# Two-operand elementwise work of the middle stage goes from GpSimd to VectorE in a hybrid decoder step

## The chip, the cores and the metric

The kernel runs on one core of one Trainium2 chip. The metric is the device time of one execution in microseconds (us). Engines are called PE (TensorE matmul), PEld (its weight load), DVE (VectorE), ACT (ScalarE), POOL (GpSimd) and SP (SyncE, which here only issues DMAs).

## The reference

One layer (`DEPTH = 1`) is applied to a prompt of 1024 tokens and to a sample group of 8 single tokens; the kernel handles them as 1032 columns of one activation matrix.

```python
xn = _rms_norm(h, W['norm_g'][l])
zall = jnp.einsum('btd,de->bte', xn, W['w_in'][l])     # 1024 -> 5760 columns
# z_shift | g_a | u | v | g_b | m_a | m_b
y_a, S, last, v = _rwkv7(z_shift, ...)                 # 8 heads x 64, scan over tokens:
#   sa = S @ aa ; S = S*w + sa bb^T + v k^T ; y = S @ r ; then group norm and a bonus term
y_b = u * _chunk_spatial(layer_norm(gelu(v)))          # causal 128x128 mixing in chunks
br_a = (y_a * silu(g_a)) @ W['w_br_a'][l]
br_b = (y_b * silu(g_b)) @ W['w_br_b'][l]
h = h + (sigmoid(m_a) * br_a + sigmoid(m_b) * br_b) @ W['w_out'][l]
h = h + sigmoid(h @ W['w_ple_gate'][l] + b) * (p @ W['w_ple'][l])
y = _rms_norm(h, W['final_g'])
```

All results are float32.

## The kernel before

**Products in two parts.** A float32 product is made of three matmuls: each operand is split into a rounded part (hi) and a residual (lo), and hi·hi, hi·lo and lo·hi are added up in PSUM (line 138). `split` (line 111) makes the parts: ACT copies the raw tile into hi, then the engine that is handed in subtracts hi from raw to give lo (line 114). A block of weights, 128 output channels by 1024 inputs, comes in two slabs of 128x512 (`load_w`, line 116): a DMA into `wraw` issued by SP, the ACT cast `whi` (line 113), and the subtraction `wlo` on POOL. Three buffers of each slab tile exist, and a block uses its two slabs through all three thirds of the columns, so the second slab of the next block finds a free buffer only when the last third of the present block has passed its first half.

**Stages.** The first stage (lines 157 to 375) normalises the input and computes the v path. The middle stage (lines 377 to 1168) holds the RWKV branch with everything else woven in. The last stage (from line 1171) is three series of blocks, `w_br_a`, `w_out` and `w_gate`.

**The middle stage.** The recurrence is cut into 4 head pairs of two halves, 8 units (`un`), each of 8 chunks of 64 tokens. For a unit `stage_e` prepares the operands: decay powers `p65`, normalised keys `kn`, the matrices `m1` (tile `m1b`, two buffers, unit by unit) and `w3`. Line 663 writes the receptance products of `m1` (`zr` times the powers), line 665 the products of the normalised key. `stage_s` solves a triangular system per chunk, all chunks side by side, in 31 steps of two short DVE instructions (`xtmp` line 737, `xg` line 739). `stage_x` finishes it. `stage_c` then walks the 8 chunks in series: two PE products `pt` (line 827), an ACT copy, PE (line 833), two ACT copies, two PE products `p3b` (line 838), and on DVE the two halves of the state update that write `vsb` for the next chunk:

```python
V.scalar_tensor_tensor(nx, p3[Q[h], i % 2, h], pc[Q[h], c:c + 1], sp[Q[h]], ALU.mult, ALU.add)
```

The next chunk's `pt` needs `vsb`. `stage_t` puts a finished unit in place. `sample` does the recurrence of the 8 single tokens. Between these steps `Stream.pump` feeds PE with the matmuls of 49 weight blocks: 41 of `w_in` (13 `z`, 4 `ga`, 8 `u`, 16 gates) and 8 half-depth ones of `w_br_b`, 90 slabs in all.

**Order.** Every engine executes its instructions in one fixed order. A planner chooses it when the program is built, by a priority (the number of the instruction in the program, much lower and so more urgent for what goes through `Boost`, line 780: the chunk walk, `stage_t`, `load_yb`) and by when it expects operands to be ready. `st.lastv` is the newest DVE instruction made through `Boost`, mostly a state update. `tc.issue_after(x)` puts instructions behind x in their engine's order, with no wait for x to finish. It was already in use for every second step of `stage_s` (line 736) and for all DVE work of `sample` (line 919).

Of the kernel before, what the change touches and what calls it, by code (L numbers as in the profile page):

```python
# [10 lines left out]
ALU = mybir.AluOpType  # L11
# [16 lines left out]
CH = 64  # L28
# [26 lines left out]
def body(tc, A):  # L55
    nc = tc.nc
    V, S, G, SY = nc.vector, nc.scalar, nc.gpsimd, nc.sync
# [3 lines left out]
    f32 = lambda ap: ap.bitcast(F32)  # L61

    with ExitStack() as top:
# [47 lines left out]
        def split(hi, lo, eng, raw=None):  # L111
            raw = f32(lo) if raw is None else raw
            S.copy(hi, raw)  # L113
            eng.tensor_tensor(lo, raw, f32(hi), ALU.subtract)  # L114

        def load_w(src, nk, pool=None):
            out = []
            for k0 in range(0, nk, 4):
                n = min(4, nk - k0)
                x = k0 if pool else ""  # L120
                hi = (pool or wp).tile([P, 4, P], F32R, tag=f"whi{x}", name="whi")[:, :n]
                lo = (pool or wp).tile([P, 4, P], F32R, tag=f"wlo{x}", name="wlo")[:, :n]
                raw = (pool or wp).tile([P, 4, P], F32, tag="wraw", name="wraw", bufs=WRAW)[:, :n]
                SY.dma_start(raw, src[:, k0:k0 + n, :])
                split(hi, lo, G, raw)
                out += [(hi[:, k], lo[:, k]) for k in range(n)]
            return out

# [28 lines left out]
        with ExitStack() as es:  # L157
# [204 lines left out]
            for g in range(4):  # L362
                st = trp.tile([P, T], F32, tag="st", name="st_mix")
# [135 lines left out]
        def zblock(b, mk):  # L499
            def gen(w):  # L500
                z = mk()
                G.memset(z[:, 0:1], 0.0)

                def ev(n, ns, ps):
                    S.copy(z[:, 1 + n * W3:1 + (n + 1) * W3], ps)
                yield from mm_block(w, xhi, xlo, ev)

                def mix():
                    G.tensor_copy(zsh[:, b], z[:, TP:TP + NB + 1])
                    if b < 12:  # L510
                        zt.setdefault(b % 4, {})[b // 4] = z
                    mu = col("mu", b)
                    for n in (2, 1, 0):
                        c0 = 1 + n * W3
                        c1 = c0 + W3
                        d = r2.tile([P, W3], F32, tag="zd", name="zd")
                        e1 = min(c1, TP + 1)
                        V.tensor_tensor(d[:, :e1 - c0], z[:, c0 - 1:e1 - 1], z[:, c0:e1], ALU.subtract)
                        if n == 2:
                            V.tensor_tensor(d[:, e1 - c0:], shs[:, b], z[:, TP + 1:], ALU.subtract)  # L520
                        V.scalar_tensor_tensor(z[:, c0:c1], d, mu, z[:, c0:c1], ALU.mult, ALU.add)
                    if b < 12:
                        G.tensor_copy(zsm[:, (1, 0, 2)[b // 4], b % 4], z[:, TP + 1:])
                    else:
                        S.activation(z[0:64, 1:], z[0:64, 1:], AF.Tanh)
                        G.tensor_copy(wdas, z[:, TP + 1:])
                        for q, x, E_ in ((Q[0], lw, V), (Q[1], la, G)):
                            oq = Q[1 - q.start // 64]
                            S.copy(x[q], z[q, 1:])
                            E_.tensor_tensor(x[oq], z[q, 1:], f32(x[q]), ALU.subtract)  # L530
                if b // 4 != 1:
                    return mix
                mix()
            j, x = b % 4, b // 4
            go = {0: lambda: st.r_seen >= 2 * j, 1: lambda: st.k_seen >= 2 * j, 2: lambda: st.c_seen >= 2 * j - 4,
                  3: lambda: True}[x]
            st.add(("z", b), b, gen, ready=go if x != 1 else lambda: st.it >= 2 * j - 3, go=go)
# [38 lines left out]
        def lora_w(j):  # L576
            js = slice(j * P, (j + 1) * P)
            raw = wp.tile([P, 4, P], F32, tag="wraw", name="lraw", bufs=WRAW)[:, :2]
            for x in range(2):
                for h in range(2):  # L580
                    SY.dma_start(raw[Q[h], x], A["wup"][x * 64:x * 64 + 64, js])
            S.copy(lhi, raw)
            for x in range(2):
                G.tensor_tensor(llo[Q[x], x], raw[Q[x], x], f32(lhi[Q[x], x]), ALU.subtract)

        sgat, zt, ut, fin_s, tl = {}, {}, {}, {}, {}
        ybh, ybl = xhi[:, 0:4], xlo[:, 0:4]
# [2 lines left out]
        def stage_e(un):  # L590
# [54 lines left out]
            V.scalar_tensor_tensor(kp, zr[:, hs], col("r_k", j), kp, ALU.mult, ALU.mult)  # L645
            rkh = re_.tile([P, HT], F32R, tag="e_i", name="e_rkh")
            rkl = re_.tile([P, HT], F32R, tag="e_a", name="e_rkl")
            split(rkh, rkl, G, kp)
            yield YE[2]
            st.until(("z", 8 + j))  # L650
            if un == 0:
# [5 lines left out]
            for b0 in (0, 4):  # L657
# [2 lines left out]
                    yield 1  # L660
                for h in range(2):
                    q = Q[h]
                    G.tensor_tensor(m1[q, cs, h, RC[h]], c64(zr[q, hs])[:, cs], p65[q, cs, 1:], ALU.mult)
                    for b in range(2):
                        (G, V)[h].tensor_tensor(kord(m1[q, cs, h, AC[h]], b), perm(c64(kn[q])[:, cs], b),
                                                perm(p65[q, cs, 0:CH], b), ALU.mult)
                if b0:
                    st.r_seen += 1
                ps = aps().rearrange("p (c h x) -> p c h x", h=2, x=CH)
# [222 lines left out]
        def ugb(j, part):  # L892
            def gen(w):
                mx = trp.tile([P, T], F32, tag="st", name="mx")
                SY.dma_start(mx, (d_mix, d_yb)[part][j])

                def ev(n, ns, ps):
                    ue = r2.tile([P, W3], F32, tag="zd", name="ue")
                    if part == 0:
                        S.activation(ue, ps, AF.Gelu_apprx_tanh)  # L900
                    else:
                        S.activation(ue, ps, AF.Tanh, scale=0.5)
                        V.scalar_tensor_tensor(ue, ue, 1.0, ps, ALU.add, ALU.mult)
                    G.tensor_tensor(mx[:, ns], mx[:, ns], ue, ALU.mult)
                yield from mm_block(w, xhi, xlo, ev)
                SY.dma_start(d_yb[j], mx)
            st.add(("u", j, part), (17 if part == 0 else 25) + j, gen)
# [20 lines left out]
        def sample():  # L928
# [83 lines left out]
            yl = sa_(P, 32, tag="s_yl")  # L1012
            for r in range(2):
                it = []
                for x, E_ in enumerate((G, V)):
                    isl, s_ = sst[2 * r + x]
                    t_ = re_.tile([P, 8, HD], F32, tag=("e_a", "e_p")[x], name="s_t")
                    sa8 = r2.tile([P, 8], F32, tag="s_sa", name="s_sa")
                    E_.tensor_tensor(t_, s_, bi(lv[:, NKK]), ALU.mult)
                    it.append((E_, isl, s_, t_, sa8))  # L1020
                yield YS[0]
                for E_, isl, s_, t_, sa8 in it:
                    V.tensor_reduce(sa8, t_, AX.X, ALU.add)
                    E_.tensor_tensor(s_, s_, bi(lv[:, WV]), ALU.mult)
                    E_.tensor_tensor(t_, bj(sa8), bi(lv[:, BV]), ALU.mult)
                    E_.tensor_tensor(s_, s_, t_, ALU.add)
                    E_.tensor_tensor(t_, bj(lvv[:, isl]), bi(lv[:, KP]), ALU.mult)
                    E_.tensor_tensor(s_, s_, t_, ALU.add)
                    E_.tensor_tensor(t_, s_, bi(lv[:, RV]), ALU.mult)
                yield YS[1]  # L1030
                for E_, isl, s_, t_, sa8 in it:
                    V.tensor_reduce(yl[:, isl], t_, AX.X, ALU.add)
                yield 1
                while r == 0 and st.cdone < 7 * HCH + 3:
                    yield 1
# [36 lines left out]
        def load_ya(n):  # L1072
            ns = slice(n * W3, min((n + 1) * W3, TP))
            st.load = SY.dma_start(f32(yal[:, :3, ns]), d_ya[:3, :, ns].rearrange("k p t -> p k t")).ins
            for k in range(3):
                st.later.append(lambda k=k, ns=ns: split(yah[:, k, ns], yal[:, k, ns], G))

        def load_yb(n):
            V, S, G_ = (Boost(e) for e in (nc.vector, nc.scalar, nc.gpsimd))
            ns = slice(n * W3, (n + 1) * W3)  # L1080
            SY.dma_start(f32(ybl[:, :, ns]), d_yb[:, :, ns].rearrange("k p t -> p k t"))
            for k in range(4):
                S.copy(ybh[:, k, ns], f32(ybl[:, k, ns]))
                (G_ if k == 1 else V).tensor_tensor(ybl[:, k, ns], f32(ybl[:, k, ns]), f32(ybh[:, k, ns]), ALU.subtract)

        def br_b(j):
            def gen(w):
# [11 lines left out]
        fill += [lambda j=j: mgate(37 + j, d_mb[j]) for j in range(KD)]  # L1099
        fill += [lambda j=j: mgate(29 + j, d_ma[j]) for j in range(KD)]  # L1100

        tc.cur_priority = 100000
        boost[0] = 50000
        zblock(12, lambda: re_.tile([P, T + 1], F32, tag="zr", name="wda"))
# [61 lines left out]
            pass  # L1166
        repool.__exit__(None, None, None)
        rw.close()
        use_pmm(4)

        tr2 = top.enter_context(tc.tile_pool(name="tr2", bufs=2))
# [219 lines left out]
```

## Time and profile before

| | us |
|---|---|
| median of 3 runs (lowest, highest) | 1077.36 (1076.85, 1077.84) |
| the profiled execution | 1079.88 |
| its span, first to last instruction | 1078.0 |
| PE busy | 1016.7 (94%) |
| PEld busy | 978.4 (91%) |
| DVE busy | 655.1 (61%) |
| ACT busy | 449.3 (42%) |
| POOL busy | 471.6 (44%) |

The profiled execution has 1.9 us outside its span. Busy time is the union of an engine's instructions. PE at 94% counts overlapping matmuls, so the idle rest is a lower bound of what PE loses. The slices of the profile page show PE at 6 to 9 tenths throughout, DVE busiest in the first two thirds, and the granted clock of PE at full speed but for single slices.

### The profile page before, as it was taken

What the parts mean: (1) busy time and instruction counts of PE and PEld (TensorE: products, weight loads), DVE (VectorE), ACT (ScalarE), POOL (GpSimd) and SP (SyncE); (2) the same over time, 40 slices, a digit from 0 to 9 for tenths busy, and PEclk for the clock granted to TensorE, in tenths of its full rate; (3) what the DMA queues carried; (4) which work ended last, traced back from release to release, by engine and by line L of the source; (5) the groups of instructions that cost most, each with busy time, mean ns of one, the idle gap of its engine ahead of it and who ended that gap; (6) DMA issues with size and microseconds to landing.
All of it is one profiled execution on the core that took longest, in us unless ns stands there. A gap on an engine that the chain in (4) does not pass through costs nothing. (4 is left out here: it accounts for less than half of the span.)

```text
span 1078.0 us, 17989 instructions
## 1 busy us (share of the span) xinstructions
PE 1016.7 (94%) x6590; PEld 978.4 (91%) x6590; DVE 655.1 (61%) x1487; ACT 449.3 (42%) x1087; POOL 471.6 (44%) x484
## 2 busy tenths in 40 slices
PE   8889999899798999989998999999899999999996
PEld 8768898899798899989998999989799999999995
DVE  6898565847648768577476583563876551114544
ACT  4531334245364453555444545434532232225431
POOL 2462665444364343343414333334943674453213
PEclk9999999999899999999998999999899999999997
DMA  9811412152224231132232332422765763224204
GB/s 277 243 51 48 145 40 58 40 131 83 79 78 151 79 86 61 47 103 56 79 110 49 105 101 70 134 86 41 266 206 179 240 231 118 79 83 133 80 1 157
DMA packets 95224, 118.72 MB, mean 110 GB/s; under 512 B 40672, under 2 KB 61024, under 8 KB 95136
## 3 DMA queue, kind: packets, MB, share of 16 engines
q1 hardware_dynamic: 95136, 117.57, 35.5%
q8 instruction: 52, 0.85, 0.3%
q14 instruction: 36, 0.29, 0.1%
HBM read 84.75 MB, written 32.25 MB: 109 GB/s over the span
## 5 line engine op out<-in xcount | busy, mean ns | idle before, releaser
L138 PE MATMUL mm<-xhi,wlo 128*128 128x344 f32 x1176 | 388.2, 330 | 8.0 <-POOL wlo L114 6.2
L138 PE MATMUL mm<-xlo,whi 128*128 128x344 f32 x1176 | 389.3, 331 | 0.9 <-DVE xlo L791 0.8
L138 PE MATMUL mm<-xhi,whi 128*128 128x344 f32 x1176 | 388.7, 331 | 0.4 <-DVE mb L1092 0.3
L114 POOL TENSOR_TENSOR wlo<-wraw,whi 128x512 fp32r<-128x512 f32 x130 | 171.2, 1319 | 217.6 <-ACT whi L113 215.6
L138 PEld LDWEIGHTS mm<-xhi,wlo 128*128 128x128 f32 x1176 | 225.1, 191 | 10.5 <-POOL wlo L114 7.3
L138 PEld LDWEIGHTS mm<-xlo,whi 128*128 128x128 f32 x1176 | 224.9, 191 | 3.0 <-DVE xlo L791 1.7
L138 PEld LDWEIGHTS mm<-xhi,whi 128*128 128x128 f32 x1176 | 224.9, 191 | 2.6 <-DVE mb L1092 0.6
L113 ACT CAST whi<-wraw 128x512 fp32r<-128x512 f32 x130 | 80.2, 619 | 61.8 <-PE mm L138 44.4
L737 DVE TENSOR_TENSOR xtmp<-nb,xg 128x48 f32<-128x48 f32 (+23 forms) x248 | 70.6, 285 | 20.4 <-DMA nb<-d_n 13.6
L739 DVE TENSOR_TENSOR xg<-xg,xtmp 128x48 f32<-128x48 f32 (+23 forms) x248 | 78.0, 315 | 7.6 <-DVE xtmp L737 0.2
L791 ACT ACTIVATE sp<-vsb,pc 64x64 f32<-64x64 f32 x128 | 44.2, 345 | 69.6 <-DVE vsb L791 67.7
L791 DVE SCALAR_TENSOR_TENSOR vsb<-p3b,pc,sp 64x64 f32<-64x64 f32 x112 | 31.6, 282 | 57.5 <-PE p3b L838 55.3
L827 PEld LDWEIGHTS pt<-vsb,m1b 128*128 128x128 f32 x256 | 37.9, 194 | 28.0 <-DVE vsb L791 27.5
L138 PE MATMUL mm<-hlo,whi 128*128 128x388 f32 (+1 forms) x192 | 62.0, 323 | 0.0
L138 PE MATMUL mm<-hhi,whi 128*128 128x388 f32 (+1 forms) x192 | 61.7, 321 | 0.0
L138 PE MATMUL mm<-hhi,wlo 128*128 128x388 f32 (+1 forms) x192 | 61.7, 321 | 0.0
L138 PE MATMUL mm<-mgl,whi 128*128 128x344 f32 x192 | 61.4, 320 | 0.2 <-POOL mgl L1188 0.2
L827 PE MATMUL pt<-vsb,m1b 128*128 128x64 f32 x256 | 40.4, 275 | 22.4 <-DVE vsb L791 22.4
L138 PE MATMUL mm<-mgh,whi 128*128 128x344 f32 x192 | 61.3, 319 | 0.0
L138 PE MATMUL mm<-mgh,wlo 128*128 128x344 f32 x192 | 61.3, 319 | 0.0
L1202 DVE SCALAR_TENSOR_TENSOR h<-mm,xres 128x344 f32<-128x344 f32 x24 | 12.4, 517 | 75.0 <-PE mm L138 72.6
L791 ACT COPY vsb<-pt 64x64 f32<-64x64 f32 x128 | 26.5, 207 | 43.7 <-PE pt L833 41.7
(297 smaller groups left out, 1881.5 us busy)
## 6 DMA issues: line engine op xcount, KB each, us to landing
wraw<-w_in SPq DMA_DIRECT2D x82, 256.0 KB, 2.8
d_ple<-st_ple SPq DMA_DIRECT2D x8, 516.0 KB, 3.4
d_yb<-mx SPq DMA_DIRECT2D x8, 516.0 KB, 2.8
d_mb<-st_m SPq DMA_DIRECT2D x8, 516.0 KB, 3.4
d_ma<-st_m SPq DMA_DIRECT2D x8, 516.0 KB, 4.1
mb<-d_mb SPq DMA_DIRECT2D x8, 516.0 KB, 4.3
d_tb<-mb SPq DMA_DIRECT2D x8, 516.0 KB, 4.9
ma<-d_ma SPq DMA_DIRECT2D x8, 516.0 KB, 5.3
```

Source lines behind the costliest of these rows:

```text
L113: S.copy(hi, raw)
L114: eng.tensor_tensor(lo, raw, f32(hi), ALU.subtract)
L138: PE.matmul(ps, l, r, start=(k == 0 and i == 0), stop=(k == nk - 1 and i == 2))
L737: V.tensor_tensor(tv, row.unsqueeze(2).broadcast_to([P, 2, na, w]), xg[:, :, :na, s:s + 1].broadcast_to([P, 2, na, w]), ALU.mult)
L739: V.tensor_tensor(xg[:, :, :na, s + 1:], xg[:, :, :na, s + 1:], tv, ALU.add)
L791: r = f(*a, **k)
L827: PE.matmul(pt[:, 0, h], m1[:, c, h], vs[:, c, h], start=True, stop=True)
L1202: V.scalar_tensor_tensor(h[:, j, ns], ps, 0.25, xr[:, ns], ALU.mult, ALU.add)
```

## The change

In the middle stage these POOL instructions with two tensor operands become DVE instructions: the weight residual `wlo` (by `sub[0] = V`, reset to `G` for the last stage), the residual of `la` (line 530), of `lhi` (584), of `rkh` (648), all products of `m1` (663 and the head of 665 that was on POOL), the product into `mx` (904), the half of the sample recurrence that was on POOL (1019 to 1029), and the residuals of `load_ya` (1076) and of one of four tiles of `load_yb` (1084). For units above 1 the product of line 663 is issued after `st.lastv`; the loop of line 665 stands outside that block. POOL keeps its powers (`rpow`), copies, memsets and the one-operand scale of line 605. No DMA and no matmul is added, removed or changed.

```diff
+        sub = [G]
+
         def load_w(src, nk, pool=None):
...
-                split(hi, lo, G, raw)
+                split(hi, lo, sub[0], raw)
...
-                        for q, x, E_ in ((Q[0], lw, V), (Q[1], la, G)):
+                        for q, x in ((Q[0], lw), (Q[1], la)):
...
-                            E_.tensor_tensor(x[oq], z[q, 1:], f32(x[q]), ALU.subtract)
+                            V.tensor_tensor(x[oq], z[q, 1:], f32(x[q]), ALU.subtract)
...
-                G.tensor_tensor(llo[Q[x], x], raw[Q[x], x], f32(lhi[Q[x], x]), ALU.subtract)
+                V.tensor_tensor(llo[Q[x], x], raw[Q[x], x], f32(lhi[Q[x], x]), ALU.subtract)
...
-            split(rkh, rkl, G, kp)
+            split(rkh, rkl, V, kp)
...
-                    G.tensor_tensor(m1[q, cs, h, RC[h]], c64(zr[q, hs])[:, cs], p65[q, cs, 1:], ALU.mult)
+                    with tc.issue_after(st.lastv) if un > 1 else ExitStack():
+                        V.tensor_tensor(m1[q, cs, h, RC[h]], c64(zr[q, hs])[:, cs], p65[q, cs, 1:], ALU.mult)
                     for b in range(2):
-                        (G, V)[h].tensor_tensor(kord(m1[q, cs, h, AC[h]], b), perm(c64(kn[q])[:, cs], b),
-                                                perm(p65[q, cs, 0:CH], b), ALU.mult)
+                        V.tensor_tensor(kord(m1[q, cs, h, AC[h]], b), perm(c64(kn[q])[:, cs], b),
+                                        perm(p65[q, cs, 0:CH], b), ALU.mult)
...
-                    G.tensor_tensor(mx[:, ns], mx[:, ns], ue, ALU.mult)
+                    V.tensor_tensor(mx[:, ns], mx[:, ns], ue, ALU.mult)
...
-                for x, E_ in enumerate((G, V)):
+                for x in range(2):
...
-                    E_.tensor_tensor(t_, s_, bi(lv[:, NKK]), ALU.mult)
+                    V.tensor_tensor(t_, s_, bi(lv[:, NKK]), ALU.mult)
...
-                    E_.tensor_tensor(s_, s_, bi(lv[:, WV]), ALU.mult)
+                    V.tensor_tensor(s_, s_, bi(lv[:, WV]), ALU.mult)
...
-                st.later.append(lambda k=k, ns=ns: split(yah[:, k, ns], yal[:, k, ns], G))
+                st.later.append(lambda k=k, ns=ns: split(yah[:, k, ns], yal[:, k, ns], V))
...
-                (G_ if k == 1 else V).tensor_tensor(ybl[:, k, ns], f32(ybl[:, k, ns]), f32(ybh[:, k, ns]), ALU.subtract)
+                V.tensor_tensor(ybl[:, k, ns], f32(ybl[:, k, ns]), f32(ybh[:, k, ns]), ALU.subtract)
...
+        sub[0] = V
         tc.cur_priority = 100000
...
         rw.close()
+        sub[0] = G
         use_pmm(4)
```

## Rows read from the trace of the kernel before

**Rows 1.** Stage view: stretch, length, busy PE, PEld, DVE, ACT, POOL; clock, DMA share, GB/s.

```profile
100.00:825.00 725.00, 683.52 (x4604) 660.96 (x4603) 472.82 (x1145) 330.62 (x876) 317.64 (x342) 0.98 0.33 97
...
```

**Rows 2.** Waits of PE, 100 to 825: who for whom, us, times, longest.

```profile
PE pt L827 <- DVE vsb L791: 22.4, 19, 5.5
PE mm L138 <- POOL wlo L114: 6.2, 4, 2.4
PE aa L671 <- DVE e_bk L641: 3.7, 1, 3.7
PE mm L138 <- POOL zr L502: 1.8, 1, 1.8
...
PE aa L607 <- POOL la L530: 1.1, 1, 1.1
...
```

**Rows 3.** Granted clock around one long wait, by stage view.

```profile
274.00:290.00 16.00, 10.49 (x53) 10.14 (x52) 10.90 (x23) 4.78 (x15) 6.32 (x7) 0.79 0.37 112
```

**Rows 4.** Timeline of DVE from 336 us: start, duration, engine, line, tiles, shapes.

```profile
...
336.11 1.22 DVE L739 TENSOR_TENSOR xg<-xg,xtmp 128x92 f32<-128x92 f32 x1
...
338.61 0.25 DVE L739 TENSOR_TENSOR xg<-xg,xtmp 128x88 f32<-128x88 f32 x1
...
343.11 0.59 DVE L791 SCALAR_TENSOR_TENSOR vsb<-p3b,pc,sp 64x64 f32<-64x64 f32 x2
...
```

**Rows 5.** Timeline of POOL in the same stretch.

```profile
335.82 2.66 POOL L114 TENSOR_TENSOR wlo<-wraw,whi 128x512 fp32r<-128x512 f32 x2 [1.25 <-ACT whi L113]
...
```

**Rows 6.** Single tiles on DVE: count, then shortest/median/longest in ns.

```profile
L791 DVE SCALAR_TENSOR_TENSOR vsb<-p3b,pc,sp x112: 266/284/295, 250.4 to 808.1; 64x64 f32<-64x64 f32 x112
...
L665 DVE TENSOR_TENSOR m1b<-e_kn,e_p x32: 384/788/1976, 150.6 to 670.8; 64x128 f32<-64x128 f32 x32
...
L737 DVE TENSOR_TENSOR xtmp<-nb,xg x248: 163/222/1320, 188.6 to 725.7; 128x48 f32<-128x48 f32 x12, 128x54 f32<-128x54 f32 x8, 128x84 f32<-128x84 f32 x8, 128x56 f32<-128x56 f32 x8
L739 DVE TENSOR_TENSOR xg<-xg,xtmp x248: 166/224/2174, 190.3 to 725.9; 128x48 f32<-128x48 f32 x12, 128x54 f32<-128x54 f32 x8, 128x84 f32<-128x84 f32 x8, 128x56 f32<-128x56 f32 x8
...
```

**Rows 7.** Groups of the page: busy us, mean ns of one, idle before.

```profile
L737 DVE TENSOR_TENSOR xtmp<-nb,xg 128x48 f32<-128x48 f32 (+23 forms) x248 | 70.6, 285 | 20.4 <-DMA nb<-d_n 13.6
L739 DVE TENSOR_TENSOR xg<-xg,xtmp 128x48 f32<-128x48 f32 (+23 forms) x248 | 78.0, 315 | 7.6 <-DVE xtmp L737 0.2
```

**Rows 8.** Groups of DVE, shapes apart, whole span.

```profile
L665 DVE TENSOR_TENSOR m1b<-e_kn,e_p 64x128 f32<-64x128 f32 x32 | 26.1, 836 | 11.2 <-PE pt L827 10.6
...
L700 DVE TENSOR_TENSOR w3b<-aa,mka 64x256 f32<-64x256 f32 x32 | 13.3, 416 | 19.5 <-ACT nab L699 19.1
...
L114 DVE TENSOR_TENSOR wlo_v<-wrawv,whi_v 128x512 fp32r<-128x512 f32 x4 | 7.5, 1865 | 1.7 <-ACT whi_v L113 1.6
...
L903 DVE SCALAR_TENSOR_TENSOR ue<-ue,mm 128x344 f32<-128x344 f32 x12 | 6.1, 510 | 7.7 <-ACT ue L902 7.6
...
L212 DVE TENSOR_TENSOR wpl<-wpraw,wph 128x512 fp32r<-128x512 f32 x1 | 0.7, 683 | 0.0
...
```

**Rows 9.** Groups of ACT, 100 to 825.

```profile
L113 ACT CAST whi<-wraw 128x512 fp32r<-128x512 f32 x88 | 54.3, 619 | 34.5 <-PE mm L138 21.1 <-issue 8.2 <-DMA mka<-mka 1.3
```

**Rows 10.** Waits of POOL, of DVE and of SP's queue, 100 to 825.

```profile
POOL wlo L114 <- ACT whi L113: 150.8, 49, 10.2
POOL m1b L663 <- PE pt L827: 35.0, 7, 9.4
...
DVE m1b L665 <- PE pt L827: 10.6, 5, 2.4
...
SPq L124 <- POOL wlo L114: 237.8, 51, 12.6
...
```

**Rows 11.** Chain of waits, one stretch of the last stage: start, us, what.

```profile
881.20 166.99 PE mm L138 x1053
```

**Rows 12.** Timelines of POOL and of DVE from 697.5 us, one row each.

```profile
698.20 5.87 POOL L101 TENSOR_TENSOR s_pool<-s_pool,mhalf 128x16 f32<-128x16 f32 x2 [11.67 <-DVE s_pool L925]
...
698.27 0.21 DVE L739 TENSOR_TENSOR xg<-xg,xtmp 128x52 f32<-128x52 f32 x1
...
```

More of the change, by code (lines that the diff above doesn't have):

```diff
@@ L1018, in sample @@
                     sa8 = r2.tile([P, 8], F32, tag="s_sa", name="s_sa")
-                    E_.tensor_tensor(t_, s_, bi(lv[:, NKK]), ALU.mult)
-                    it.append((E_, isl, s_, t_, sa8))
+                    V.tensor_tensor(t_, s_, bi(lv[:, NKK]), ALU.mult)
+                    it.append((isl, s_, t_, sa8))
                 yield YS[0]
-                for E_, isl, s_, t_, sa8 in it:
+                for isl, s_, t_, sa8 in it:
                     V.tensor_reduce(sa8, t_, AX.X, ALU.add)
-                    E_.tensor_tensor(s_, s_, bi(lv[:, WV]), ALU.mult)
[L1025 to L1029, printed above, removed]
+                    V.tensor_tensor(s_, s_, bi(lv[:, WV]), ALU.mult)
+                    V.tensor_tensor(t_, bj(sa8), bi(lv[:, BV]), ALU.mult)
+                    V.tensor_tensor(s_, s_, t_, ALU.add)
+                    V.tensor_tensor(t_, bj(lvv[:, isl]), bi(lv[:, KP]), ALU.mult)
+                    V.tensor_tensor(s_, s_, t_, ALU.add)
+                    V.tensor_tensor(t_, s_, bi(lv[:, RV]), ALU.mult)
                 yield YS[1]
-                for E_, isl, s_, t_, sa8 in it:
+                for isl, s_, t_, sa8 in it:
                     V.tensor_reduce(yl[:, isl], t_, AX.X, ALU.add)
@@ L1075, in load_ya @@
             for k in range(3):
-                st.later.append(lambda k=k, ns=ns: split(yah[:, k, ns], yal[:, k, ns], G))
+                st.later.append(lambda k=k, ns=ns: split(yah[:, k, ns], yal[:, k, ns], V))
         def load_yb(n):
-            V, S, G_ = (Boost(e) for e in (nc.vector, nc.scalar, nc.gpsimd))
+            V, S = (Boost(e) for e in (nc.vector, nc.scalar))
             ns = slice(n * W3, (n + 1) * W3)
```

## The prediction

> **What bounds the kernel now.** I read the stage view first: PE is the fullest engine, and in the middle stage (100 to 825 us) it is busy 683.5 of 725 us while DVE is busy 472.8 and POOL 317.6 [rows 1]. So the middle stage can give back about 42 us of PE idle time, and what half clock costs. The granted clock there is 0.98 on average, which is 2% of 725 = 14.5 us lost [rows 1]; one instance is 0.79 over 16 us around a 5.5 us wait of PE, 3.4 us lost [rows 2, 3].
>
> Then the waits of PE in that stage [rows 2]: 22.4 us in 19 waits for the state update `vsb` on DVE, 6.2 us in 4 for `wlo` on POOL, 3.7 us for `e_bk` on DVE, 1.8 us for a memset on POOL, 1.1 us for `la` on POOL; together 35.2 us.
>
> Then why `vsb` is late. The update itself never is slow: 266 to 295 ns in all 112 [rows 6]. What stands in front of it on DVE is. At 336.11 a solve step takes 1.22 us while POOL makes two `wlo` (335.82 to 338.48), and one right after 0.25 us [rows 4, 5]; the steps behind it run on until that chunk's update starts at 343.11. Over the stage a step's median is 222 and 224 ns but its mean 285 and 315 [rows 6, 7], and the DVE products of line 665 take 384 ns at best, 836 on average, 1976 at worst [rows 6, 8]. So two-operand instructions on DVE stand still while POOL runs one of its own. These three groups alone lose 248 x 0.063 + 248 x 0.091 + 32 x 0.452 = 15.6 + 22.6 + 14.5 = 52.7 us of DVE time.
>
> **The rule weighed against the trace.** The row first: under two POOL powers that run 5.87 us from 698.20, the solve step at 698.27 takes 0.21 us, as the fastest of its kind do [rows 6, 12]. The Trainium skill, page "SBUF — State Buffer", section "Who interferes with whom", says that a DVE instruction with two SBUF inputs and a GpSimd one that reads SBUF exclude each other, the later one blocked for the whole instruction. The `wlo` rows agree; the powers do not. By the page these two powers could have held DVE for up to 5.87 us, and the POOL work that stays would keep part of the gain back; by the row they held it for nothing, and my sum goes by the row.
>
> **The change part by part.** Added to DVE, at the price without a POOL partner:
> - 90 `wlo` at 0.683 us, the same shape and operation [rows 8]: 61.5 us. The other bound is the four `wlo_v` on DVE at 1.865, 168 us [rows 8]; those ran in the first stage with POOL making residuals beside them, and that partner is what goes. I take the low one.
> - 32 products of line 663, 64x256, at 0.416 (nearest row, line 700 [rows 8]): 13.3 us.
> - 32 of line 665 at 0.384, the shortest of the same instruction [rows 6]: 12.3 us.
> - 24 `mx` and 12 residuals of `load_ya`/`load_yb`, 344 wide, at 0.510 [rows 8]: 18.4 us.
> - 8 `rkl` and 12 sample instructions, 128x512, at 0.683: 13.7 us; 8 `llo` at no more than 0.384, and `la` as two of 0.683: 4.4 us.
>
> Sum 123.6 us, less at least the 52.7 above: DVE goes from 473 to at most 544 us, 75% of the stage. It has room; the question is only who waits in its order. POOL keeps powers, copies, memsets and one scale.
>
> What comes back on PE:
> - `vsb`: 22.4 us. The excess of one stretched step, 1.22 - 0.25 = 0.97 us [rows 4], is near a mean wait of 22.4/19 = 1.2 us; the 5.5 us one needs several. With no partner on POOL I leave a third, 7.4, for updates that find other DVE work running: 15.0 back. Bounds: 0 and 22.4.
> - `wlo`: 6.2 us. The longest, 2.4, I put down to the two powers [rows 12], behind which a residual stood on POOL; that cause goes. 4.0 back; bounds 6.2 back and the third rival.
> - `e_bk`: the same stretching of the DVE work ahead of it; 2.0 of 3.7.
> - the memset and `la`: POOL becomes nearly free, `la` is made at DVE's speed; 2.5 of 2.9.
>
> 23.5 us. In the instance shown the clock fell behind a long wait of PE [rows 3], so I let its 14.5 us shrink in the share of PE's 42 us idle that goes: 14.5 x 23.5/42 = 8 back.
>
> What is lost. The new wait is `wlo` on DVE for the ACT cast. On POOL 49 such waits take 150.8 us, 3.1 us each, and cost nothing because nothing urgent queues there [rows 10]. On DVE a state update, solve steps and the evacuations by DVE queue behind, and PE's `pt` waits for the update. I don't expect 3.1 us each: DVE's order has other work to put in front. What a slab can hold is about its cast, 0.619 [rows 9], and itself, 0.683, or 1.3 us; 90 slabs in 725 us make that 16% of the time; 10 of 64 updates are caught, 0.65 us each, 6.7 us, and with the clock in its proportion (14.5/42) 9 us. Bounds: 0, and the third rival. `wlo` also frees `wraw`, for which SP's queue waits 237.8 us in 51 waits [rows 10]; behind a held weight load stand the loads of `stage_s`. That wait is there today and only changes the engine that ends it; I cost it at nothing while `wlo` is no later than today.
>
> The hold puts the receptance products (units 2 to 7) behind the newest update. They free no one earlier; behind them stand the key products and later the `m1` matmuls. On POOL these products waited 35.0 us in 7 waits for `pt` [rows 10], and in front of an update that would be ruinous; behind it `pt` of that chunk is past. I cost the hold at nothing, with the second rival as its other end.
>
> Net: 23.5 + 8 - 9 = 22.5 us less. The profiled execution was 1079.88 (span 1078.0 and 1.9 around it), so it becomes 1057.4; the median of the runs shown lies 2.5 us lower: 1055.
>
> **The rivals.**
> 1. DVE's order is as full as before, and updates find `wlo` where they found stretched steps. Only the waits on POOL return: 4.0 + 2.5, with clock 8.7, against 9 lost: 1077. For it: 123.6 us added against 52.7 seen removed. Against: a `wlo` is 0.683, half of the 1.3 it used to block.
> 2. The hold doesn't do what its description says: it covers line 663, and the key products of line 665 are outside it. Those on DVE wait 10.6 us for `pt` today, in 5 waits [rows 10]; with twice as many and each in front of an update, 10.6 more and its clock share, 14 us: 1069. Against: DVE was idle in those waits, and no PE wait names them.
> 3. Slower: residuals come late for PE. The second slab of a block gets its buffer 24 matmuls before PE needs it, 24 x 0.1586 = 3.8 us [rows 11]; less cast and residual 2.5 us are left. A unit's preparation now puts on DVE in one run four 128x512 instructions, `rkl`, and two plus four products of `m1`: 5 x 0.683 + 2 x 0.416 + 4 x 0.384 = 5.8 us, 3.3 too much; a unit's tail with `stage_t`, some six of 0.683, 4.1 us, 1.6 too much. Eight of each: 39 us, with the clock 53, against 31.5 returned: 1077.4 + 21 = 1099. It decides from 31.5/53, that is when 6 in 10 of these runs catch a slab. For it: PE waits for POOL's `wlo` today without such runs. Against: residuals are spread over the time in which nothing is boosted, and the first slab of a block has a whole block's lead.
>
> **How the numbers follow.** Forecast 0.50, with its own range 1040 to 1068; rival 1 0.17; rival 2 0.13; rival 3 0.20, spread from 1080 to 1100. Below lies the case that all of the 35.2 us and 12 of clock return, 1030. The range 1036 to 1086 leaves out about 6 in 100 below and 11 above. A measurement of this kernel tells about 0.2% (2.2 us) from no change. Faster: the forecast, 0.11 of rival 2, 0.05 of rival 1, 0.01 of the third: 0.67. Same: 0.11. Slower: 0.22.
>
> **What would show it.** Right: solve steps and line 665 with means within 30 ns of their medians; waits of PE for `vsb` under 10 us; POOL under 100 us in the stage; `wlo` at 0.68 us on DVE; clock of the stage at 0.99. Rival 1: the same clean durations but waits for `vsb` at 20 us. Rival 2: DVE `m1b` waiting over 20 us for `pt`. Rival 3: waits of PE for DVE `wlo` well over 10 us. Wrong altogether would be solve steps still stretched with POOL empty.

## The result, and the profile after

| | before | after |
|---|---|---|
| median (lowest to highest) | 1077.11 us (1075.77 to 1077.84, 4 runs) | 1037.78 us (1035.79 to 1038.12, 4 runs) |
| the profiled execution | 1079.88 | 1035.79 |
| its span | 1078.0 | 1034.0 |

The ratio is 0.9632, 95% interval 0.9616 to 0.9649: 39.3 us less, where 22.5 were forecast. A later set of runs gave 0.9589 (0.957 to 0.9608) for the same kernel. Line numbers have moved by two or three in the middle stage and by five in the last (line 663 is 666 now, 665 is 668, 138 is 140, 827 is 830, 791 is 794); in the kernels of the experiments they differ from these by up to five.

The stage view, the middle stage cut where its first matmul starts and where the last unit's rows are put in place, split where the first unit's walk begins. Columns as in [rows 1]. Before:

```profile
96.00:243.00 147.00, 137.64 (x906) 132.13 (x905) 91.93 (x188) 54.76 (x120) 72.84 (x92) 0.99 0.29 85
243.00:824.00 581.00, 548.85 (x3718) 531.50 (x3717) 384.00 (x963) 275.63 (x755) 245.52 (x251) 0.98 0.33 99
```

After:

```profile
92.00:232.00 140.00, 135.18 (x908) 130.92 (x908) 96.54 (x233) 54.73 (x120) 24.55 (x46) 1.00 0.30 88
232.00:779.00 547.00, 533.96 (x3722) 520.20 (x3722) 393.85 (x1136) 277.38 (x756) 57.94 (x79) 1.00 0.36 107
```

The same 4624 to 4630 matmuls take 687 us for 728. PE is idle for 17.9 us of them (4.8 + 13.0) where it was for 41.5 (9.4 + 32.2), and the clock is granted in full in both parts (1.00, where it was 0.99 and 0.98). DVE is busy 490 us for 476, with 218 more instructions in all: nearly everything that it took over is paid by what no longer stretches. POOL goes from 318 to 82 us. The last stage takes what it took (254 us before, 255 after).

The waits of PE, which answer to [rows 2]: us in total, times, longest.

```profile
PE mm L140 <- DVE wlo L114: 4.0, 3, 1.6
PE pt L830 <- DVE vsb L794: 3.3, 7, 0.9
PE aa L696 <- ACT vsb L686: 2.3, 4, 0.8
PE pt L836 <- ACT e L794: 1.9, 5, 0.6
PE aa L1063 <- DVE s_ys L928: 1.7, 1, 1.7
...
```

The wait for the state update falls from 22.4 to 3.3 us, its longest from 5.5 to 0.9; `e_bk`, the memset and `la` are gone. The single tiles on DVE, shortest/median/longest in ns, answer to [rows 6]:

```profile
L794 DVE SCALAR_TENSOR_TENSOR vsb<-p3b,pc,sp x112: 267/284/294, 239.9 to 762.7; 64x64 f32<-64x64 f32 x112
L668 DVE TENSOR_TENSOR m1b<-e_kn,e_p x64: 365/392/422, 144.9 to 634.1; 64x128 f32<-64x128 f32 x64
L666 DVE TENSOR_TENSOR m1b<-zr,e_p x32: 405/420/423, 141.7 to 640.6; 64x256 f32<-64x256 f32 x32
...
L742 DVE TENSOR_TENSOR xg<-xg,xtmp x248: 164/219/278, 182.4 to 685.5; 128x48 f32<-128x48 f32 x12, 128x54 f32<-128x54 f32 x8, 128x84 f32<-128x84 f32 x8, 128x56 f32<-128x56 f32 x8
...
```

No solve step takes more than 278 ns (2174 before), no product of `m1` by the key more than 422 (1976 before). The groups of DVE in the stage (busy us, mean ns | idle before), which answer to [rows 7, 8]:

```profile
L114 DVE TENSOR_TENSOR wlo<-wraw,whi 128x512 fp32r<-128x512 f32 x87 | 59.7, 689 | 27.8 <-ACT whi L113 26.8
...
L742 DVE TENSOR_TENSOR xg<-xg,xtmp 128x48 f32<-128x48 f32 (+23 forms) x248 | 54.2, 219 | 6.2
...
L668 DVE TENSOR_TENSOR m1b<-e_kn,e_p 64x128 f32<-64x128 f32 x64 | 24.1, 392 | 8.1 <-PE pt L830 7.4
L666 DVE TENSOR_TENSOR m1b<-zr,e_p 64x256 f32<-64x256 f32 x32 | 13.3, 416 | 0.5
...
```

A residual costs DVE 0.689 us (0.683 was used), line 666 exactly the 0.416 used, line 668 0.392 for 0.384. The waits of DVE, which answer to its row in [rows 10]:

```profile
DVE vsb L794 <- PE p3b L841: 31.3, 26, 4.1
DVE wlo L114 <- ACT whi L113: 26.8, 26, 3.1
...
DVE m1b L668 <- PE pt L830: 7.4, 5, 2.2
```

DVE now waits for the casts, as POOL did, and still is early for 26 updates.

### The profile page after: what moved, and what is told of

It reads as the page before. It is cut to its first block, busy times and chain, and to the rows that moved or that the text cites. A ratio compares the mean times of both kernels' runs of the same rounds, so it can differ in the third digit from the quotient of the medians.

```text
span 1034.0 us, 17897 instructions
## 1 busy us (share of the span) xinstructions
PE 998.7 (97%) x6590; PEld 966.2 (93%) x6590; DVE 665.0 (64%) x1708; ACT 450.9 (44%) x1087; POOL 232.1 (22%) x263
## 5 line engine op out<-in xcount | busy, mean ns | idle before, releaser
L140 PE MATMUL mm<-xhi,wlo 128*128 128x344 f32 x1176 | 383.5, 326 | 4.0 <-DVE wlo L114 4.0
L140 PE MATMUL mm<-xhi,whi 128*128 128x344 f32 x1176 | 384.6, 327 | 0.1
L140 PE MATMUL mm<-xlo,whi 128*128 128x344 f32 x1176 | 384.3, 327 | 0.1
L140 PEld LDWEIGHTS mm<-xhi,wlo 128*128 128x128 f32 x1176 | 221.6, 188 | 5.6 <-DVE wlo L114 4.9
L140 PEld LDWEIGHTS mm<-xhi,whi 128*128 128x128 f32 x1176 | 221.6, 188 | 1.9 <-DVE mb L1095 0.5
L140 PEld LDWEIGHTS mm<-xlo,whi 128*128 128x128 f32 x1176 | 221.4, 188 | 1.8 <-DVE xlo L794 0.4
L114 POOL TENSOR_TENSOR wlo<-wraw,whi 128x512 fp32r<-128x512 f32 x40 | 52.9, 1322 | 122.9 <-ACT whi L113 122.5
L114 DVE TENSOR_TENSOR wlo<-wraw,whi 128x512 fp32r<-128x512 f32 x90 | 61.7, 689 | 27.8 <-ACT whi L113 26.8
L740 DVE TENSOR_TENSOR xtmp<-nb,xg 128x48 f32<-128x48 f32 (+23 forms) x248 | 54.1, 218 | 15.0 <-DMA nb<-d_n 8.9
L742 DVE TENSOR_TENSOR xg<-xg,xtmp 128x48 f32<-128x48 f32 (+23 forms) x248 | 54.2, 219 | 6.2
L794 DVE SCALAR_TENSOR_TENSOR vsb<-p3b,pc,sp 64x64 f32<-64x64 f32 x112 | 31.7, 283 | 33.8 <-PE p3b L841 31.3
```

The lines of the kernel that those rows point to most:

```text
L140: PE.matmul(ps, l, r, start=(k == 0 and i == 0), stop=(k == nk - 1 and i == 2))
L740: V.tensor_tensor(tv, row.unsqueeze(2).broadcast_to([P, 2, na, w]), xg[:, :, :na, s:s + 1].broadcast_to([P, 2, na, w]), ALU.mult)
L742: V.tensor_tensor(xg[:, :, :na, s + 1:], xg[:, :, :na, s + 1:], tv, ALU.add)
L794: r = f(*a, **k)
```

## The experiments

Theory: two-operand instructions of POOL and DVE stop each other; DVE falls behind its fixed order, and state updates and other work that PE waits for come late. Rivals: POOL itself was late or slow; the hold made the difference; the later or earlier release of the weight buffers did. Ratios are to the kernel before, run beside it in the same set.

| kernel | us | ratio | 95% interval |
|---|---|---|---|
| after, again | 1036.45 | 0.9589 | 0.957 to 0.9608 |
| POOL reads beside | 1072.01 | 0.9907 | 0.9871 to 0.9943 |
| POOL writes beside | 1032.23 | 0.9541 | 0.951 to 0.9573 |
| POOL powers beside | 1043.42 | 0.9648 | 0.9616 to 0.968 |
| `wlo` alone moved | 1048.71 | 0.9701 | 0.9674 to 0.9728 |
| all but `wlo` moved | 1044.84 | 0.9678 | 0.9639 to 0.9716 |
| the same, DVE loaded | 1077.97 | 0.9985 | 0.9964 to 1.0006 |
| no hold | 1034.64 | 0.957 | 0.9546 to 0.9593 |
| hold for both products | 1039.45 | 0.9618 | 0.96 to 0.9637 |
| hold for `wlo` | 1035.95 | 0.9589 | 0.9556 to 0.9622 |
| last stage too | 1034.92 | 0.9592 | 0.9544 to 0.964 |
| scale and `gz` too | 1036.93 | 0.9605 | 0.9567 to 0.9643 |

**POOL busy beside DVE, in three ways.** Nothing waits for what is added, except the next DMA into the raw tile and, with the reads, the next residual into the same `wlo` tile.

```diff
                 split(hi, lo, sub[0], raw)
+                if sub[0] is V:
+                    G.tensor_tensor(raw, raw, f32(lo), ALU.mult)          # reads beside
+                    for _ in range(3): G.memset(raw, 0.0)                 # or: writes beside
+                    G.tensor_tensor(raw[:, 0, :8], onesq, raw[:, 0, :8], ALU.pow)   # or: powers
```

> The changed kernel, and behind each of the 90 residuals that DVE now makes POOL multiplies the same two tiles (raw by lo) into raw, which nothing reads afterwards. Theory (two-operand instructions of POOL and DVE stop each other, so DVE falls behind its order): stretched DVE instructions come back without any wait for POOL, solve steps again with maxima over 1 us, waits of PE for the state update over 10 us; 1050 to 1075 us. Rival (POOL's lateness was the cost, not its presence): nothing on the path waits for the added work; 1036 to 1041. Second rival (the added work frees the raw buffers about 1.3 us later, and late weight loads cost the time): slower by the same amount as the run with writes only.

> As the run with reads beside, but POOL fills raw three times with zeros (it writes and reads no operand), about 1.5 us per slab and the raw buffer held as long. Theory: no stretched DVE instructions; 1036 to 1042 us. Rival (late weight loads): the same time as the run with reads beside, whatever it is. If a write by POOL stops DVE too, solve steps show maxima over 0.5 us.

> As the run with reads beside, but POOL raises 8 columns of ones to the power of 8 columns of raw, about 1.7 us per slab, two operands read but few elements. From the powers of the kernel before, under which solve steps took 0.21 us: POOL busy for 150 us more and the time 1036 to 1042. If an instruction of POOL that reads stops DVE for its whole duration, however few elements it reads: 1055 to 1080.

The three added groups on POOL from 92 to 820 us, reads, writes and powers (busy us, mean ns | idle before):

```profile
L129 POOL TENSOR_TENSOR wraw<-wraw,wlo 128x512 f32<-128x512 f32 x87 | 120.9, 1392 | 342.4 <-DVE wlo L114 226.5 <-issue 90.7 <-DVE xg L744 13.0
```

```profile
L130 POOL MEMSET wraw<- 128x512 f32 x261 | 136.5, 526 | 303.2 <-DVE wlo L114 255.4 <-issue 25.6 <-ACT vsb L797 7.8
```

```profile
L132 POOL TENSOR_TENSOR wraw<-onesq,wraw 128x8 f32<-128x8 f32 x87 | 150.7, 1735 | 310.3 <-DVE wlo L117 148.8 <-issue 110.1 <-DVE xg L747 27.9
```

The longest solve steps (`xg`) in the same order:

```profile
L744 DVE TENSOR_TENSOR xg<-xg,xtmp x248: 167/220/1348, 190.5 to 716.6; 128x48 f32<-128x48 f32 x12, 128x54 f32<-128x54 f32 x8, 128x84 f32<-128x84 f32 x8, 128x56 f32<-128x56 f32 x8
```

```profile
L745 DVE TENSOR_TENSOR xg<-xg,xtmp x248: 168/219/395, 184.0 to 688.1; 128x48 f32<-128x48 f32 x12, 128x54 f32<-128x54 f32 x8, 128x84 f32<-128x84 f32 x8, 128x56 f32<-128x56 f32 x8
```

```profile
L747 DVE TENSOR_TENSOR xg<-xg,xtmp x248: 168/220/255, 184.9 to 694.0; 128x48 f32<-128x48 f32 x12, 128x54 f32<-128x54 f32 x8, 128x84 f32<-128x84 f32 x8, 128x56 f32<-128x56 f32 x8
```

POOL is busy for 121, 137 and 151 us more, at the same places, and only the first stretches DVE much: the longest `xg` is 1348 ns, against 395 and 255. The powers and the writes did run beside DVE: 113 solve steps overlap an added power in the trace and 124 an added memset, none over 260 ns. The 395 ns come from something else. POOL copies `nab` into `gz` then, one operand read, and the steps beside these copies take 0.33 to 0.40 us:

```profile
233.23 1.78 POOL L767 COPY gz<-nab 32x128 f32<-32x128 f32 x4 [5.33 <-PE aa L770]
```

```profile
233.91 0.33 DVE L745 TENSOR_TENSOR xg<-xg,xtmp 128x62 f32<-128x62 f32 x1
234.26 0.40 DVE L743 TENSOR_TENSOR xtmp<-nb,xg 128x60 f32<-128x60 f32 x1
234.70 0.40 DVE L745 TENSOR_TENSOR xg<-xg,xtmp 128x60 f32<-128x60 f32 x1
235.12 0.22 DVE L743 TENSOR_TENSOR xtmp<-nb,xg 128x58 f32<-128x58 f32 x1
```

So it isn't the two operands on POOL's side that stop DVE; a copy that reads one does it too.

Between reads and writes lie 0.9907 - 0.9541 = 3.7%, 40 us, as much as the whole change brought. That is the theory shown: the presence of POOL's reads costs, with nobody waiting for their result. The second rival (later release of the weight buffers) can be no more than a part of it. SP's queue waits for POOL to leave the raw tile in all three, for 228, 176 and 200 us:

```profile
SPq L126 <- POOL wraw L129: 228.5, 54, 12.9
```

```profile
SPq L126 <- POOL wraw L130: 175.8, 55, 11.6
```

```profile
SPq L129 <- POOL wraw L132: 200.4, 50, 12.5
```

Two points of the expectations missed. The powers took 1043.42 us, not 1036 to 1042, and are 11 us slower than the writes beside them, with no solve step stretched; PE waits 4.0 us in front of line 771, in part for the load of `xa`, where it was 0.7 in the changed kernel:

```profile
PE aa L771 <- issue: 2.2, 2, 1.3
PE aa L771 <- DMA xa<-d_x: 1.8, 1, 1.8
```

So a busy POOL costs something by another way, which stays open, and 29 us (reads against powers) to 40 us (reads against writes) are what reading costs. And with the reads, the waits of PE for the state update are 7.7 us and not over 10:

```profile
PE pt L832 <- DVE vsb L796: 7.7, 11, 1.9
PE mm L142 <- DVE wlo L114: 4.3, 3, 1.6
PE aa L768 <- DMA xa<-d_x: 3.4, 2, 2.9
PE aa L698 <- ACT vsb L688: 3.0, 4, 1.3
PE aa L684 <- DVE zv L525: 2.9, 1, 2.9
PE aa L698 <- DVE zv L693: 2.7, 1, 2.7
...
```

The loss is spread over much that hangs on DVE, not on the update alone. That the writes came out faster than the changed kernel (0.9541 against 0.9632 and 0.9589 in other sets) stays open: their profiled span, 1033.8 us, is no shorter than the 1034.0 of the changed kernel, and their four times go with the granted clock, from 1029.56 us at 0.996 to 1035.62 at 0.988.

**Each half alone.** First the residual alone, `sub[0] = V` in the kernel before; then the changed kernel without that line.

> The kernel before with only the weight residuals of the middle stage on DVE; all else stays on POOL, and there is no hold. Theory: wlo is 116 of some 240 us of POOL's two-operand work there, so about half to two thirds of the gain: 1050 to 1062 us, solve steps partly stretched still by the products of m1 and mx. Rival (PE waited for POOL's wlo, 6.2 us with a share of the clock): 1067 to 1072.

> The changed kernel, but the weight residuals of the middle stage stay on POOL; all else on DVE. Theory: the 116 us of wlo on POOL go on stopping DVE, the other 125 us of two-operand work no longer do, so what is left of the gain is 8 to 20 us: ratio 0.981 to 0.993, solve steps with maxima of 1.2 us and more. Rival (the two halves count for the same, as their POOL time does): half the gain, 0.978 to 0.982.

Both missed on the same side: 0.9701 and 0.9678, each alone brings about three quarters of the gain or more (3.0 and 3.2% of 3.7 to 4.1). The halves don't add up, so the cost of blocking is not in proportion to its amount. In the second, POOL's `wlo` still stretch the solve steps, and it costs 0.5 to 0.9% against the two sets of the changed kernel; in the run with reads beside as many POOL reads cost 3 to 4%.

```profile
L742 DVE TENSOR_TENSOR xg<-xg,xtmp x248: 168/220/1314, 188.2 to 698.9; 128x48 f32<-128x48 f32 x12, 128x54 f32<-128x54 f32 x8, 128x84 f32<-128x84 f32 x8, 128x56 f32<-128x56 f32 x8
```

What differs between these two is DVE's own load, by the 62 us of `wlo`, and what POOL's reads follow: the cast here, DVE's residual there.

**Blocking with DVE loaded.** All but `wlo` moved, and DVE gets 62 us of work behind each of POOL's residuals:

```diff
-                split(hi, lo, sub[0], raw)
+                split(hi, lo, G, raw)
+                if sub[0] is V:
+                    V.tensor_tensor(raw, raw, f32(lo), ALU.mult)
```

> The run with all but wlo moved, and behind each of POOL's 90 residuals of the middle stage DVE multiplies raw by lo into raw, which nothing reads: DVE carries as much as in the changed kernel (62 us more), POOL reads as much as in the run with reads beside, and PE waits only for POOL's residual. Theory (blocking costs by what DVE has no room to catch up: the same blocking costs 9 us with DVE light and 33 with it loaded): ratio 0.980 to 0.995. Rival (the run with reads beside was slow because DVE's own residuals were blocked and came late to PE): no loss beyond the run with all but wlo moved, 0.964 to 0.972.

0.9985: nothing is left of the gain, above the 0.980 to 0.995 that the theory gave. PE does not wait longer for residuals; it waits for DVE:

```profile
PE pt L832 <- DVE vsb L796: 16.9, 16, 5.1
PE aa L698 <- ACT vsb L688: 3.5, 4, 1.1
PE aa L684 <- DVE m1b L707: 3.0, 1, 3.0
PE aa L684 <- DVE zv L525: 2.9, 1, 2.9
PE aa L676 <- DVE e_bk L645: 2.7, 1, 2.7
...
PE mm L142 <- POOL wlo L114: 2.0, 3, 0.9
```

But this run changes more than DVE's load. The added work needs POOL's residual, so DVE, in its fixed order, now waits for POOL, its largest wait in the stage:

```profile
DVE wraw L129 <- POOL wlo L114: 47.9, 29, 6.2
```

Such waits can make updates late by themselves, so the run does not show that load and blocking alone take the gain. The run with reads beside has no such wait, and its own rival, residuals that come late to PE, is answered by its rows: 4.3 us in 3 waits, against 4.0 in 3 in the changed kernel.

The stage views of these kernels from 92 to 820 us: all but `wlo` moved, reads beside, DVE loaded, writes beside, each with DVE's busy time third and the clock behind POOL's:

```profile
92.00:820.00 728.00, 704.57 (x4831) 685.02 (x4830) 504.44 (x1319) 341.21 (x896) 215.32 (x227) 1.00 0.36 107
```

```profile
92.00:820.00 728.00, 690.22 (x4650) 667.16 (x4649) 545.52 (x1379) 334.48 (x882) 203.31 (x213) 0.98 0.33 98
```

```profile
92.00:820.00 728.00, 686.12 (x4642) 662.64 (x4641) 538.74 (x1378) 331.20 (x876) 206.10 (x213) 0.98 0.33 97
```

```profile
92.00:820.00 728.00, 711.98 (x4898) 694.14 (x4897) 515.27 (x1415) 345.98 (x904) 241.53 (x409) 1.00 0.36 111
```

PE is idle for 23, 38, 42 and 16 us in them. Two per cent of the clock over 728 us are another 14.5, so of the 27 to 33 us by which the two slow kernels lie behind the run with all but `wlo` moved, about half is TensorE's clock and half its waits.

Of four corners three are measured: with the 62 us on DVE and without these reads on POOL, 0.954 to 0.965 (powers and writes beside included); with reads and without the 62 us, 0.968; with both, 0.991 and 0.9985. A kernel with neither is not among them, so what the load costs alone is not shown. That the price of the reads grows with DVE's load fits the three, but it rests on the run with reads beside, and it is not shown apart from what else differs. In the kernel before, DVE is not that loaded (476 us), but POOL's reads are twice as many, and PE waits on POOL's results as well.

**The hold.** Taken away; widened to the key products; put on `wlo`:

```diff
-                    with tc.issue_after(st.lastv) if un > 1 else ExitStack():
+                    with ExitStack():
...
+                with tc.issue_after(st.lastv) if sub[0] is V and hasattr(st, "lastv") else ExitStack():
+                    split(hi, lo, sub[0], raw)
```

> The changed kernel without the hold. Theory (the gain is the end of mutual blocking, the hold costs and brings next to nothing): within 4 us of the changed kernel. Rival (the hold carries the gain: without it the products of line 666 stand in front of a state update and wait for pt, as they did for 35 us on POOL): 15 us or more slower, and DVE waits for pt in front of m1b go from 7.4 to over 25 us.

> The changed kernel with the key products of line 668 inside the hold too. Theory: within 3 us of the changed kernel, DVE m1b waits for pt gone from 7.4 to under 2 us. Rival 2 of the prediction (the unheld key products hold up updates): 5 to 14 us faster.

> The changed kernel with each weight residual of the middle stage issued behind the newest state update. If residuals that wait for their cast (26.8 us in 26 waits) hold up updates, as the term of 9 us in the prediction has it: 3 to 9 us faster, PE waits for the update under 2 us. If those waits lie where DVE had nothing urgent: no faster, and slower by as much as PE waits longer for residuals (0 to 10 us).

> The changed kernel once more, beside the others of this set, so that differences under 1% can be read on one chip: ratio 0.960 to 0.967 to the kernel before.

Against the changed kernel beside them (0.9589) the three are 0.957, 0.9618 and 0.9589. The hold of the change is worth nothing: without it DVE waits for `pt` in front of `m1b` for 7.4 us in 5 waits, as with it, and those waits only go from line 668 to line 666. Held for both products, as the change's description reads, they vanish, and the kernel is no faster (0.3% slower). Holding `wlo`, and its cast with it, leaves its waits for the cast as they were (28.4 us) and the time too: the 9 us that the prediction set for them aren't there to be saved.

**Further moves.**

> The changed kernel with the two-operand work of the last stage on DVE too (wlo, mgl, hlo; about 100 us of POOL time). Theory: stretching costs only where a wait of PE ends on DVE; in the last stage PE waits for the two engines under 4 us in all, so within 3 us of the changed kernel although DVE's stretched instructions vanish there. Rival (every us of mutual blocking counts): 5 us or more faster.

> The changed kernel without the hold and with two more one-operand instructions of POOL on DVE, the scale in front of the scan (8, for which DVE waits 10.9 us) and the copies into gz (32, 16 us of POOL). Theory: PE does not wait for either, so the same within 3 us, perhaps 1 to 2 us faster by the scale. If POOL's one-operand reads still stop DVE noticeably: 3 us or more faster.

0.9592 and 0.9605: no difference to the changed kernel in either (the second also goes without the hold). In the last stage DVE's instructions become clean (`mgl`, `hlo` and `ma` 511 to 515 ns on average, where `ma` took 596 in the changed kernel), and PE waits in it for two things, as before:

```profile
PE fst L1252 <- ACT gq L1233: 2.1, 2, 1.5
PE fbc L1266 <- POOL fms L101: 1.0, 1, 1.0
```

In this stage, where PE waits 3.1 us in all, the blocking cost nothing that can be measured. Apart from the writes beside, left open above, no version beats the changed kernel by more than its own two sets differ.

## Why the prediction was right, and where it was too small

The direction, the cause and the place were as forecast, and the time lies inside the range, 1.8 us from its lower end; the gain is 1.75 times the 22.5 us of the sum. The time lies below the 1040 to 1068 that the prediction gave its forecast, towards the case in which everything returns (1030). That it is still inside the range owes something to luck. Point by point:

- **What bounds the kernel.** Right: of the 44 us by which the profiled executions differ, 41 are in the middle stage, and nearly all of them in its idle time (23.6) and its clock (about 13 to 14.5).
- **DVE's load.** 123.6 us added against at least 52.7 removed gave at most 544 us. Measured 490: with all groups counted, what went was about 110, twice what the three groups of the sum show, as the pricing of the added work held where it is shown (0.689, 0.416, 0.392). The bound was safe but far.
- **PE's waits.** By terms, `vsb` gave 19.1 us back (15.0 forecast), `wlo` 2.2 (4.0), `e_bk` 3.7 (2.0), the memset and `la` 2.9 (2.5): 27.9 in all, where 23.5 were forecast. All other waits of PE grew, from 6.2 to 10.0 us. So idle time fell from 41.5 to 17.9 us, by 23.6; that this is the forecast's 23.5, which had no such loss in it, is luck.
- **The loss.** The first mis-sized term: 9 us (6.7 and their share of the clock) for residuals that stand in front of an update. DVE does wait 26.8 us for casts, in 26 waits. But PE's waits for the update are 3.3 us in all, from every cause, where the sum kept 7.4 and added 6.7; and holding the residuals behind the updates changed nothing. DVE has room there: in front of updates it waits 31.3 us for PE even now. What was lost is the 3.8 us by which the other waits grew (`aa` for `vsb`, `s_ys` and `zv`, `pt` for `e`).
- **The clock.** The other one: it was let shrink in proportion, 8 of 14.5 us back. It came back whole in the profiled execution, 1.00 in both parts of the stage, with 18 us of idle time left. The longest wait left is 1.7 us. In the stretch of [rows 3] PE stood still for 5.5 us and then ran at the lower of its two levels (1.2 of 2.4 GHz, 0.50 in the view):

```profile
284.00:286.00 2.00, 2.00 (x9) 1.94 (x9) 1.24 (x7) 0.46 (x2) 0.00 (x0) 0.50 0.35 140
```

That long waits bring the fall fits this, and a proportion was the wrong form; what exactly decides stays open. In the run without the hold the stretch from 732 to 744 us shows 0.86, while the waits of PE ahead of it, three rows of 0.6, 0.6 and 0.3 us from 725 to 740, are the same as in the changed kernel, where the clock held:

```profile
732.00:744.00 12.00, 10.63 (x60) 10.02 (x59) 7.48 (x18) 4.81 (x15) 0.00 (x0) 0.86 0.68 239
```

- With the measured terms the sum is 27.9 - 3.8 + 14.5 = 38.6, near the 39.3 of the medians (the 14.5 is an estimate from a clock of two digits; by the two parts above it is 13). The 44 of the profiled executions hold about 3 more in front of the stage, whose first matmul comes at 92 us and not at 96; the run with all but `wlo` moved does not have them. Why stays open.
- **The hold** was rightly costed at nothing. **Rival 2** wanted over 20 us of `m1b` waiting for `pt`: 7.4 are there, less than the 10.6 of before, and taking them away brought nothing. **Rival 1** had the load right (DVE busy 490 us for 476) but not what follows: updates wait 3.3 us at that load, not 20, once nothing is stretched. **Rival 3**: PE waits for residuals 4.0 us in 3 waits of up to 1.6, so long runs of DVE caught a slab three times at most, where ten would have decided for it.
- **The rule weighed.** Going by the row was right: with 150.7 us of powers added on POOL no solve step takes over 260 ns. Where the Trainium skill ("SBUF — State Buffer", section "Who interferes with whom") has a DVE instruction with two SBUF inputs and a GpSimd one that reads SBUF block each other, the measurement decides against it for powers of 8 columns. Where the same section of the Trainium skill says that a GpSimd instruction that only writes does not block, the run with writes agrees: no step beside a memset is over 260 ns.

## What to carry to other kernels

Where short DVE instructions of one kind have a mean well above their median and some take five times as long, look at what POOL does at those times before adding up loads: an engine with room to spare can be made late by its neighbour, and moving the neighbour's wide reads of SBUF onto it can leave it hardly busier (490 us for 476 here). The price of such blocking isn't its length: removing either half of it brought about three quarters of the gain here, and TensorE's clock was part of the price. That it grows with the load of the engine that is stopped fits these runs, without being shown by them. Blocking in a stage where PE waits for neither engine may stay.

## What the runs showed of the hardware that was not expected

An instruction of POOL of 1735 ns with two operands of 8 columns (a power) does not stop DVE at all, one of 1392 ns with two operands of 512 columns up to 1.1 us (1348 against 220 ns), and a copy of about 0.4 us that reads one operand of 128 columns up to 0.2 us (397 against 220 ns). So how long POOL is busy doesn't tell how long DVE is stopped. Stops go with DVE's two-operand reads of SBUF: the state update, which takes one operand from PSUM, was never stretched, at 295 ns at most before and 294 after.
